# Row sums of 1024 columns: VectorE takes over the body, and the last row is divided differently

## The chip, the cores and the metric

The kernel runs on one core of a Trainium2 chip. The metric is the device time of one execution in microseconds (us). All times quoted are medians of fast runs; every run of this study was in the fast state, and the granted clock was 1.0 in all of them. One core does all the work, so there is no second core to compare with.

A profile shows one execution. Its span (162.4 us) is about 1.8 us shorter than the device time of the same execution. Below, DVE is VectorE, ACT is ScalarE, SP is SyncE, whose queue issues the loads and the store, and "landing" is the moment when the last of a load's 16 semaphore increments arrives (the core has 16 DMA engines, and the packet records show one increment behind each of 16 strings of packets). Where the text gives a landing that no copied line shows, it was read from the semaphore records of the trace.

## The reference

```python
x = np.random.randn(32, 512, 1024).astype(np.float32)     # 67.1 MB
out = np.sum(x, axis=-1)                                  # 32 x 512, 64 KB
```

There is one addition for each 4 bytes that are read. The 16384 rows are divided over 128 partitions, 128 rows on each.

## The kernel before

Eight tiles of 16 rows per partition (8.39 MB each) pass through a pool of three buffers. Each whole tile is divided equally: VectorE reduces rows 0 to 7 in one instruction, ScalarE sums rows 8 to 15 one by one, with a copy that also accumulates. The eighth tile is loaded in ever smaller pieces, so that little work is left when the last data land.

```python
xpool = ctx.enter_context(tc.tile_pool(name="x", bufs=3))
# ... cut: rows_dve = tensor_reduce over n rows; rows_act = one activation with accum_out per row
for t in range(T - 1):                       # seven whole tiles
    c0 = t * G
    xt = xpool.tile([P, G * D], F32, tag="xt", name="xt")
    load(xt, c0, 0, G * D)
    rows_dve(xt, c0, 0, G // 2)
    rows_act(xt, c0, G // 2, G // 2)
# ... cut: the last tile is loaded as 8, 4, 2 and 1 rows; then the last row as 512, 256 and 256 columns
for j, n in runs:
    if n > 1:
        rows_dve(xt, c0, j, n // 2)
        rows_act(xt, c0, j + n // 2, n // 2)
    else:
        rows_act(xt, c0, j, 1)
acc = [part[:, 0:1], part[:, 1:2], res[:, C - 1 : C]]
for i, (a, b) in enumerate(zip(cuts, cuts[1:])):     # three pieces of the last row, in a chain
    pairs_dve(xt, a, b, acc[i - 1] if i else 0.0, acc[i])
nc.sync.dma_start(out=out2d, in_=res)
```

`pairs_dve` is a `tensor_tensor_reduce`: it adds the two halves of a piece element by element and accumulates the sums. Each of the three calls starts from the result of the one before.

Of the kernel before, what the change touches and what calls it, by code (L numbers as in the profile page):

```python
# [1 line left out]

# [4 lines left out]

F32 = mybir.dt.float32
ADD = mybir.AluOpType.add


@with_exitstack
def kernel(
    ctx: ExitStack,
    tc: tile.TileContext,
    x: bass.AP,
    out: bass.AP,
):
    nc = tc.nc
    P = nc.NUM_PARTITIONS  # L20

    x_flat = x.flatten_outer_dims()
    R, D = x_flat.shape
    assert R % P == 0
    C = R // P

    x_p = x_flat.rearrange("(p c) d -> p (c d)", p=P)
    out2d = out.rearrange("a (b c) -> (a b) c", c=C)

    G = 16  # L30
    assert C % G == 0
    T = C // G

    xpool = ctx.enter_context(tc.tile_pool(name="x", bufs=3))
    rpool = ctx.enter_context(tc.tile_pool(name="res", bufs=1))
    res = rpool.tile([P, C], F32, name="res")
    part = rpool.tile([P, 4], F32, name="part")

    def load(xt, c0, a, b):
        nc.sync.dma_start(out=xt[:, a:b], in_=x_p[:, c0 * D + a : c0 * D + b])  # L40

    def rows_dve(xt, c0, j, n):
        nc.vector.tensor_reduce(  # L43
            out=res[:, c0 + j : c0 + j + n],
            in_=xt[:, j * D : (j + n) * D].rearrange("p (j d) -> p j d", d=D),
            axis=mybir.AxisListType.X,
            op=ADD,
        )

    def rows_act(xt, c0, j, n):  # L50
        for i in range(j, j + n):
            v = xt[:, i * D : (i + 1) * D]
            nc.scalar.activation(  # L53
                out=v,
                in_=v,
                func=mybir.ActivationFunctionType.Copy,
                accum_out=res[:, c0 + i : c0 + i + 1],
            )

    def pairs_dve(xt, a, b, first, acc):  # L60
        h = (b - a) // 2
        nc.vector.tensor_tensor_reduce(  # L62
            out=xt[:, a : a + h],
            in0=xt[:, a : a + h],
            in1=xt[:, a + h : b],
            scale=1.0,
            scalar=first,
            op0=ADD,
            op1=ADD,
            accum_out=acc,  # L70
        )

    for t in range(T - 1):
        c0 = t * G
        xt = xpool.tile([P, G * D], F32, tag="xt", name="xt")
        load(xt, c0, 0, G * D)
        rows_dve(xt, c0, 0, G // 2)
        rows_act(xt, c0, G // 2, G // 2)

    c0 = (T - 1) * G  # L80
    xt = xpool.tile([P, G * D], F32, tag="xt", name="xt")
    j = 0
    runs = []
    for n in (8, 4, 2, 1):
        load(xt, c0, j * D, (j + n) * D)
        runs.append((j, n))
        j += n
    cuts = [j * D + k for k in (0, D // 2, 3 * D // 4, D)]
    for a, b in zip(cuts, cuts[1:]):
        load(xt, c0, a, b)  # L90

    for j, n in runs:
        if n > 1:
            rows_dve(xt, c0, j, n // 2)
            rows_act(xt, c0, j + n // 2, n // 2)
        else:
            rows_act(xt, c0, j, 1)
    acc = [part[:, 0:1], part[:, 1:2], res[:, C - 1 : C]]
    for i, (a, b) in enumerate(zip(cuts, cuts[1:])):
        pairs_dve(xt, a, b, acc[i - 1] if i else 0.0, acc[i])  # L100

    nc.sync.dma_start(out=out2d, in_=res)


# [1 line left out]
_INS = ['x']  # L106
_OUTS = [((32, 512), 'float32')]


# [23 lines left out]
```

## Time and profile before

| kernel before | value | where it is read |
|---|---|---|
| time | 163.97 us (163.91 to 164.00, 4 runs) | runs |
| DMA in the chain that ended last | 85% | page |
| VectorE, ScalarE busy | 43%, 43% | page |
| time per whole tile in the stream | 19.4 us for 8.39 MB | windows |
| last data landed | 159.12 us | semaphore records |
| output store issued | 159.93 us | timeline |

These are two parts of the page, busy time by engine and the chain of work that ended last:

```profile
DVE 69.9 (43%) x16; ACT 69.0 (43%) x129; POOL 0.2 (0%) x4
...
DMA 85%; DVE 11%; SPq 1%; issue 1%; DVEq 0%
```

Both compute engines are idle for more than half of the time, and the chain is made of loads. The windows view over three whole tiles (columns: window and its length, busy time of each engine with its instructions, clock, DMA share, GB/s) tells the rate:

```profile
61.94:81.30 19.36, 8.69 (x1) 8.43 (x16) 0.00 (x0) 1.00 1.00 433
81.30:100.70 19.40, 8.69 (x1) 8.43 (x16) 0.00 (x0) 1.00 1.00 433
100.70:120.07 19.37, 8.69 (x1) 8.43 (x16) 0.00 (x0) 1.00 1.00 433
```

The 16 DMA engines are busy throughout (DMA share 1.00). In the packet records of this profile a 64 KB packet takes 2.42 us (median of 896; none took less than 2.415 us), and 16 x 64 KB in 2.42 us are 433 GB/s. So the body of the kernel waits for its loads, and these run without a gap. That they could not run faster is not shown by this.

What remains is the end. This is the timeline of the last 4 us, lines of ScalarE cut (columns: start, duration, engine, line, operation, operands; in brackets the idle time before it and what ended it):

```profile
156.55 1.22 DVE L43 TENSOR_REDUCE res<-xt 128x1 f32<-128x1024 f32 x1 [0.21 <-DMA xt<-in_x_dram]
...
158.64 0.42 DVE L62 CUSTOM_DVE_ANT_0 xt<-xt 128x256 f32<-128x256 f32 x1 [0.87 <-DMA xt<-in_x_dram]
...
159.11 0.35 DVE L62 CUSTOM_DVE_ANT_0 xt<-xt,part 128x128 f32<-128x128 f32 x1
159.38 0.08 DVE L62 DVE_READ_ACCUMULATOR2_ANT part<- 128x1 f32 x1
159.50 0.35 DVE L62 CUSTOM_DVE_ANT_0 xt<-xt,part 128x128 f32<-128x128 f32 x1
159.78 0.08 DVE L62 DVE_READ_ACCUMULATOR2_ANT res<- 128x1 f32 x1
159.93 0.35 SPq L102 DMA_DIRECT2D out_dram<-res  x1
```

The three chained operations on the last row start at 158.64, 159.11 and 159.50 us. The last data landed at 159.12, so the third operation started 0.38 us after its data were there, because it waited for the second.

### The profile page before, as it was taken

What the parts mean: (1) busy time and instruction counts of PE and PEld (TensorE: products, weight loads), DVE (VectorE), ACT (ScalarE), POOL (GpSimd) and SP (SyncE); (2) the same over time, 40 slices, a digit from 0 to 9 for tenths busy, and PEclk for the clock granted to TensorE, in tenths of its full rate; (3) what the DMA queues carried; (4) which work ended last, traced back from release to release, by engine and by line L of the source; (5) the groups of instructions that cost most, each with busy time, mean ns of one, the idle gap of its engine ahead of it and who ended that gap; (6) DMA issues with size and microseconds to landing.
All of it is one profiled execution on the core that took longest, in us unless ns stands there. A gap on an engine that the chain in (4) does not pass through costs nothing.

```text
span 162.4 us, 220 instructions
## 1 busy us (share of the span) xinstructions
DVE 69.9 (43%) x16; ACT 69.0 (43%) x129; POOL 0.2 (0%) x4
## 2 busy tenths in 40 slices
DVE  0000039700595007940099101990049700697882
ACT  3000039700594007930099101990039600696881
POOL 0000000000000000000000000000000000000000
DMA  7979989989989989989997997997997997999980
GB/s 258 517 323 452 517 355 420 517 371 404 501 355 436 517 371 404 517 371 404 517 452 325 517 468 307 517 468 323 501 484 323 484 484 307 452 420 408 418 350 20
DMA packets 2161, 67.18 MB, mean 414 GB/s; under 512 B 240, under 2 KB 624, under 8 KB 880
## 3 DMA queue, kind: packets, MB, share of 16 engines
q1 hardware_dynamic: 2160, 67.18, 96.3%
q14 instruction: 1, 0.01, 0.0%
HBM read 67.11 MB, written 0.07 MB: 414 GB/s over the span
## 4 chain that ended last, share of the span: by engine, by line
DMA 85%; DVE 11%; SPq 1%; issue 1%; DVEq 0%
DMA xt<-in_x_dram 85%; DVE res L43 11%; SPq L40 1%; DVE xt L62 0%; DVE part L62 0%; DVEq L62 0%; DVEq L128 0%
## 5 line engine op out<-in xcount | busy, mean ns | idle before, releaser
L43 DVE TENSOR_REDUCE res<-xt 128x8 f32<-128x8192 f32 (+3 forms) x10 | 68.7, 6873 | 89.0 <-DMA xt<-in_x_dram 89.0
L53 ACT ACTIVATE xt<-xt 128x1024 f32<-128x1024 f32 x64 | 66.7, 1043 | 89.3 <-DMA xt<-in_x_dram 89.1
L53 ACT ACTIVATION_READ_ACCUMULATOR xt<-xt 128x1 f32 x64 | 11.9, 187 | 0.0
L53 ACT ACT_TABLE_LOAD x1 | 1.3, 1283 | 0.7 <-PEq L117 0.7
L62 DVE CUSTOM_DVE_ANT_0 xt<-xt 128x256 f32<-128x256 f32 x1 | 0.4, 425 | 0.9 <-DMA xt<-in_x_dram 0.9
L62 DVE CUSTOM_DVE_ANT_0 xt<-xt,part 128x128 f32<-128x128 f32 x2 | 0.7, 352 | 0.1
L62 DVE DVE_READ_ACCUMULATOR2_ANT part<- 128x1 f32 x2 | 0.2, 82 | 0.0
L117 POOL MEMSET const-bfloat16-1.0<- 128x1 bf16 x1 | 0.1, 101 | 0.0
L117 POOL MEMSET const-uint8-127<- 128x1 uint8 x1 | 0.1, 101 | 0.0
L117 POOL MEMSET const-float32-0.0<- 128x1 f32 x1 | 0.1, 98 | 0.2 <-issue 0.2
L117 POOL MEMSET const-float32-1.0<- 128x1 f32 x1 | 0.1, 98 | 0.0
L62 DVE DVE_READ_ACCUMULATOR2_ANT res<- 128x1 f32 x1 | 0.1, 84 | 0.0
## 6 DMA issues: line engine op xcount, KB each, us to landing
xt<-in_x_dram SPq DMA_DIRECT2D x1, 4096.0 KB, 39.7
xt<-in_x_dram SPq DMA_DIRECT2D x1, 2048.0 KB, 44.2
xt<-in_x_dram SPq DMA_DIRECT2D x1, 1024.0 KB, 46.2
xt<-in_x_dram SPq DMA_DIRECT2D x1, 512.0 KB, 47.0
xt<-in_x_dram SPq DMA_DIRECT2D x1, 256.0 KB, 47.1
xt<-in_x_dram SPq DMA_DIRECT2D x2, 128.0 KB, 43.0
xt<-in_x_dram SPq DMA_DIRECT2D x7, 49.4
out_dram<-res SPq DMA_DIRECT2D x1, 64.0 KB, 1.5
```

The lines of the kernel that those rows point to most:

```text
L40: nc.sync.dma_start(out=xt[:, a:b], in_=x_p[:, c0 * D + a : c0 * D + b])
L43: nc.vector.tensor_reduce(out=res[:, c0 + j : c0 + j + n], in_=xt[:, j * D : (j + n) * D].rearrange("p (j d) -> p j d", d=D), axis=mybir.A ...
L53: nc.scalar.activation(out=v, in_=v, func=mybir.ActivationFunctionType.Copy, accum_out=res[:, c0 + i : c0 + i + 1],)
L62: nc.vector.tensor_tensor_reduce(out=xt[:, a : a + h], in0=xt[:, a : a + h], in1=xt[:, a + h : b], scale=1.0, scalar=first, op0=ADD, op1=A ...
L117: nc = _bacc.Bacc("TRN2", target_bir_lowering=False, num_devices=1)
```

## The change

VectorE sums whole tiles alone, with 16 rows in one instruction, and ScalarE joins only in the last whole tile (6 of 16 rows) and in the last tile. The last row is loaded in two pieces, 640 and 384 columns. VectorE and ScalarE each sum 320 columns of the first; their two partial sums are stored right behind the row's last column, so that one last VectorE reduction over 384 + 2 columns finishes the row. The intent: one chained operation fewer after the last landing.

```diff
-    for t in range(T - 1):
-        ...
-        rows_dve(xt, c0, 0, G // 2)
-        rows_act(xt, c0, G // 2, G // 2)
+        while c < whole:
+            ...
+            a = ACT_ROWS if final and c + m == whole else 0      # ACT_ROWS = 6
+            rows_dve(xt, res, 0, m - a, c)
+            rows_act(xt, res, m - a, a, c + m - a)
     # ... cut: the loads of 8, 4, 2 and 1 rows stay
-    cuts = [j * D + k for k in (0, D // 2, 3 * D // 4, D)]
-    for a, b in zip(cuts, cuts[1:]):
-        load(xt, c0, a, b)
+    nc.sync.dma_start(out=tail[:, 0:CUT], in_=x_b[:, last : last + CUT])      # CUT = 640
+    nc.sync.dma_start(out=tail[:, CUT:D], in_=x_b[:, last + CUT : last + D])
     # ... cut: rows of the last tile, divided as before; row 126 now goes to VectorE as 512 pairs
-    for i, (a, b) in enumerate(zip(cuts, cuts[1:])):
-        pairs_dve(xt, a, b, acc[i - 1] if i else 0.0, acc[i])
+    nc.vector.tensor_reduce(
+        out=tail[:, D : D + 1], in_=tail[:, 0 : CUT // 2], axis=X, op=ADD
+    )
+    sum_act(tail[:, CUT // 2 : CUT], tail[:, D + 1 : D + 2])
+    nc.vector.tensor_reduce(
+        out=res[:, n - 1 : n], in_=tail[:, CUT : D + 2], axis=X, op=ADD
+    )
```

More of the change, by code (lines that the diff above doesn't have):

```diff
@@ L9 @@
 ADD = mybir.AluOpType.add
+COPY = mybir.ActivationFunctionType.Copy
+X = mybir.AxisListType.X
+BLOCKS = (128,)
+G = 16
+ACT_ROWS = 6
+CUT = 640
 @with_exitstack
@@ L23 @@
     R, D = x_flat.shape
-    assert R % P == 0
     C = R // P
-    x_p = x_flat.rearrange("(p c) d -> p (c d)", p=P)
-    out2d = out.rearrange("a (b c) -> (a b) c", c=C)
-    G = 16
-    assert C % G == 0
-    T = C // G
+    assert R % P == 0 and sum(BLOCKS) == C
+    out_flat = out.rearrange("a (b c) -> (a b c)", c=1)
     xpool = ctx.enter_context(tc.tile_pool(name="x", bufs=3))
     rpool = ctx.enter_context(tc.tile_pool(name="res", bufs=1))
-    res = rpool.tile([P, C], F32, name="res")
@@ L37, with rows_dve @@
-    part = rpool.tile([P, 4], F32, name="part")
-    def load(xt, c0, a, b):
-        nc.sync.dma_start(out=xt[:, a:b], in_=x_p[:, c0 * D + a : c0 * D + b])
-    def rows_dve(xt, c0, j, n):
+    tail = rpool.tile([P, D + 2], F32, name="tail")
+    def rows_dve(xt, res, j, n, c):
         nc.vector.tensor_reduce(
-            out=res[:, c0 + j : c0 + j + n],
+            out=res[:, c : c + n],
             in_=xt[:, j * D : (j + n) * D].rearrange("p (j d) -> p j d", d=D),
-            axis=mybir.AxisListType.X,
+            axis=X,
@@ L47, in rows_dve @@
             op=ADD,
         )
-    def rows_act(xt, c0, j, n):
-        for i in range(j, j + n):
-            v = xt[:, i * D : (i + 1) * D]
-            nc.scalar.activation(
-                out=v,
-                in_=v,
-                func=mybir.ActivationFunctionType.Copy,
-                accum_out=res[:, c0 + i : c0 + i + 1],
-            )
-    def pairs_dve(xt, a, b, first, acc):
-        h = (b - a) // 2
-        nc.vector.tensor_tensor_reduce(
-            out=xt[:, a : a + h],
-            in0=xt[:, a : a + h],
-            in1=xt[:, a + h : b],
-            scale=1.0,
-            scalar=first,
-            op0=ADD,
-            op1=ADD,
-            accum_out=acc,
-        )
@@ L73 @@
-    for t in range(T - 1):
-        c0 = t * G
-        xt = xpool.tile([P, G * D], F32, tag="xt", name="xt")
-        load(xt, c0, 0, G * D)
-        rows_dve(xt, c0, 0, G // 2)
-        rows_act(xt, c0, G // 2, G // 2)
-    c0 = (T - 1) * G
-    xt = xpool.tile([P, G * D], F32, tag="xt", name="xt")
-    j = 0
-    runs = []
-    for n in (8, 4, 2, 1):
-        load(xt, c0, j * D, (j + n) * D)
-        runs.append((j, n))
-        j += n
-    cuts = [j * D + k for k in (0, D // 2, 3 * D // 4, D)]
@@ L89, with sum_act @@
-    for a, b in zip(cuts, cuts[1:]):
-        load(xt, c0, a, b)
-    for j, n in runs:
-        if n > 1:
-            rows_dve(xt, c0, j, n // 2)
-            rows_act(xt, c0, j + n // 2, n // 2)
-        else:
-            rows_act(xt, c0, j, 1)
-    acc = [part[:, 0:1], part[:, 1:2], res[:, C - 1 : C]]
-    for i, (a, b) in enumerate(zip(cuts, cuts[1:])):
-        pairs_dve(xt, a, b, acc[i - 1] if i else 0.0, acc[i])
-    nc.sync.dma_start(out=out2d, in_=res)
+    def sum_act(v, acc):
+        nc.scalar.activation(out=v, in_=v, func=COPY, accum_out=acc)
@@ new lines, in rows_act, with row_pairs_dve, block @@
+    def rows_act(xt, res, j, n, c):
+        for i in range(n):
+            sum_act(xt[:, (j + i) * D : (j + i + 1) * D], res[:, c + i : c + i + 1])
+    def row_pairs_dve(xt, res, j, c):
+        h = D // 2
+        a, b = xt[:, j * D : j * D + h], xt[:, j * D + h : (j + 1) * D]
+        nc.vector.tensor_tensor_reduce(
+            out=a, in0=a, in1=b, scale=1.0, scalar=0.0, op0=ADD, op1=ADD,
+            accum_out=res[:, c : c + 1],
+        )
+    def block(r0, n):
+        x_b = x_flat[r0 : r0 + P * n].rearrange("(p c) d -> p (c d)", p=P)
+        out_b = out_flat[r0 : r0 + P * n].rearrange("(p c) -> p c", p=P)
+        return x_b, out_b, rpool.tile([P, n], F32, name=f"res{r0}")
@@ new lines @@
+    r0 = 0
+    for b, n in enumerate(BLOCKS):
+        x_b, out_b, res = block(r0, n)
+        r0 += P * n
+        final = b == len(BLOCKS) - 1
+        whole = n - G - (n % G if final and n % G else 0) if final else n
+        c = 0
+        while c < whole:
+            m = min(G, whole - c)
+            xt = xpool.tile([P, G * D], F32, tag="xt", name="xt")
+            nc.sync.dma_start(out=xt[:, 0 : m * D], in_=x_b[:, c * D : (c + m) * D])
+            a = ACT_ROWS if final and c + m == whole else 0
+            rows_dve(xt, res, 0, m - a, c)
+            rows_act(xt, res, m - a, a, c + m - a)
+            c += m
+        if not final:
+            nc.scalar.dma_start(out=out_b, in_=res)
@@ new lines @@
+    xt = xpool.tile([P, G * D], F32, tag="xt", name="xt")
+    first = n - c - 8
+    cuts = [0, first, first + 4, first + 6, first + 7]
+    for i, k in zip(cuts, cuts[1:]):
+        nc.sync.dma_start(out=xt[:, i * D : k * D], in_=x_b[:, (c + i) * D : (c + k) * D])
+    last = (n - 1) * D
+    nc.sync.dma_start(out=tail[:, 0:CUT], in_=x_b[:, last : last + CUT])
+    nc.sync.dma_start(out=tail[:, CUT:D], in_=x_b[:, last + CUT : last + D])
+    for i, k in zip(cuts[:2], cuts[1:3]):
+        h = (k - i + 1) // 2
+        rows_dve(xt, res, i, h, c + i)
+        rows_act(xt, res, i + h, k - i - h, c + i + h)
@@ L106 @@
+    i = cuts[2]
+    rows_dve(xt, res, i, 1, c + i)
+    rows_act(xt, res, i + 1, 1, c + i + 1)
+    row_pairs_dve(xt, res, i + 2, c + i + 2)
+    nc.vector.tensor_reduce(
[5 more added lines that the diff above has]
+    )
+    nc.sync.dma_start(out=out_b, in_=res)
 _INS = ['x']
```

## The prediction

The sum along VectorE ends at 159.75 to 160.1 us against 159.85 before, so -0.10 to +0.25 us. Earlier landing would have taken up to 0.1 us off that; with this term the net was put at -0.3 to +0.3 us and the time at 163.85 us. The 267 ns in the pair operation are 256 columns at the fitted 1.067 us for 1024, an estimate.

> **What bounds the kernel now.** The DMA stream. The page's chain that ended last is 85% DMA, and DVE and ACT are each busy only 43%. In the timeline of VectorE the whole 16-row tiles start reducing at 42.27, 61.96, 81.33, 100.73, 120.09 and 139.44 us: (139.44 - 42.27)/5 = 19.43 us for 8.39 MB, so 432 GB/s. [...] Before each tile VectorE idles about 10.7 us, waiting for the load. Only what precedes the first load (about 2 us) and what follows the last landing can change.
>
> **Body.** VectorE's durations for 8, 4, 2 and 1 rows (8686, 4420, 2286, 1220 ns) fit 1.067 us a row plus 0.153 us. Sixteen rows are then an estimated 17.22 us, under the 19.43 us cadence. The 56 ScalarE rows of the seven body tiles become 6. The buffer is returned 17.2 us after a landing and not 8.7, but with three buffers there is still about 2 us of the next tile plus a whole tile (19.4 us) queued at that moment, so the stream should not starve. I expect issue-to-landing of a body load to fall from 49.4 to about 41 us and the cadence to stay at 19.4 us. [...]
>
> **Tail.** Now: the first piece of the last row releases VectorE at 158.47 us, its three chained pieces start at 158.64, 159.11 and 159.50 and end at 159.85, 1.4 us after that landing; the output is issued at 159.93 and the span ends at 162.4. After: VectorE is fully occupied from 139.44 on. Ten rows estimated 10.8 us (to 150.2), then 4 rows (to 154.6, landed at 154.05), 2 rows (to 156.8-157.0), 1 row (to 157.9-158.2), the pair op over 512 columns (425 ns for 256 plus 267, about 0.7 us and 0.1 for the accumulator, to 158.7-159.0), 320 columns (0.49 us, to 159.2-159.5), and the final 386 columns (0.56 us): end at 159.75 to 160.1. ScalarE's 320 columns [...] are done by about 159.2 and hide beside it. So the serial chain after the last data loses an op, but the 10-row share of VectorE leaves a small backlog that returns the gain. [...] Net: between -0.3 and +0.3 us, with the output store (about 2.5 us to the end) unchanged.
>
> **Prediction.** 163.85 us (before 163.96), 8 in 10 between 163.4 and 164.3. Chance of faster by over 2%: 0.01; within 2%: 0.98; slower by over 2%: 0.01.
>
> **What would show it.** VectorE busy near 134 us (about 82% of the span), ScalarE near 15 us; 16-row reduces of 17.2 us about 19.4 us apart, idle about 2.2 us between them, released by DMA; mean GB/s unchanged at about 414; in the last 20 us VectorE with almost no idle time from the 10-row op to the last, and the last VectorE op ending within 0.3 us of 159.85. If VectorE shows idle before the last op released by DMA or ScalarE, the backlog reading is wrong.
>
> **What would make it wrong.** The DMA queues running short because buffers come back 8.5 us later (cadence over 19.6 us, idle slices in the DMA row); sixteen-row reduces slower than fitted, over 19.4 us, which would make VectorE the bound; DMA speeding up without ScalarE's traffic; a backlog larger than reckoned, pushing the end over 160.2 us.

## The result

| | before | changed |
|---|---|---|
| time, us (runs) | 163.97 (163.91 to 164.00, 4) | 164.04 (163.91 to 164.13, 4) |
| ratio | | 1.0004, 95% interval 0.9987 to 1.0022 |
| last data landed, us | 159.12 | 159.14 |
| last VectorE operation on the row, start and duration, us | 159.50, 0.35 | 159.29, 0.55 |
| output store issued, us | 159.93 | 159.87 |

A ratio here is the mean time of one kernel's runs over that of the other's runs of the same rounds, so it is not quite the ratio of the medians. The result is 0.2 us from the predicted 163.85 us.

The same two parts of the page, for the changed kernel:

```profile
DVE 123.5 (76%) x14; ACT 15.8 (10%) x29; POOL 0.2 (0%) x4
...
DMA 75%; DVE 22%; SPq 1%; ACT 0%; issue 0%; ACTq 0%
```

VectorE does 1.8 times the work, ScalarE less than a quarter. VectorE's share of the chain rose from 11% to 22%, but this is not a new bound. The chain follows a load back to its issue, and the issue to the reduction that freed the buffer; that wait is in the chain although two other loads were queued meanwhile. The windows decide, over the same stretches:

```profile
61.94:81.30 19.36, 17.22 (x1) 0.00 (x0) 0.00 (x0) 1.00 1.01 433
81.30:100.70 19.40, 17.22 (x1) 0.00 (x0) 0.00 (x0) 1.00 1.00 432
100.70:120.07 19.37, 17.22 (x1) 0.00 (x0) 0.00 (x0) 1.00 1.00 433
```

The rate is the same with a 16-row reduction of 17.22 us beside it and no ScalarE work at all: 48 ScalarE instructions fewer in these three stretches changed it by nothing that can be read (432 to 433 GB/s against 433), and a 64 KB packet takes 2.42 us as before (median of 896).

The end of the changed kernel (in the first line four reductions, of 10, 4, 2 and 1 rows, are merged; lines of ScalarE before 158 us cut):

```profile
139.49 18.46 DVE L40 TENSOR_REDUCE res<-xt 128x10 f32<-128x10240 f32 x4 [2.12 <-DMA xt<-in_x_dram]
158.00 0.69 DVE L57 CUSTOM_DVE_ANT_0 xt<-xt 128x512 f32<-128x512 f32 x1
158.62 0.08 DVE L57 DVE_READ_ACCUMULATOR2_ANT res<- 128x1 f32 x1
158.69 0.47 ACT L48 ACTIVATE tail<-tail 128x320 f32<-128x320 f32 x1 [0.95 <-DMA tail<-in_x_dram]
158.69 0.49 DVE L102 TENSOR_REDUCE tail<-tail 128x1 f32<-128x320 f32 x1
159.07 0.19 ACT L48 ACTIVATION_READ_ACCUMULATOR tail<-tail 128x1 f32 x1
159.29 0.55 DVE L106 TENSOR_REDUCE res<-tail 128x1 f32<-128x386 f32 x1
159.87 0.35 SPq L109 DMA_DIRECT2D out_dram<-res  x1
```

The last operation starts 0.21 us earlier than its counterpart before (159.29 against 159.50), and it is 0.20 us longer (0.55 against 0.35). Its start has three conditions that fall close together: VectorE ends its 320 columns at 158.69 + 0.49 = 159.18, ScalarE's accumulator is read by 159.07 + 0.19 = 159.26, and the last load landed at 159.14. The chain view names ScalarE as the last of the three, and behind it the landing of the first piece at 158.67, for which ScalarE had been idle (a q behind an engine's name stands for its sequencer):

```profile
119.89 38.78 DMA tail<-in_x_dram
158.67 0.02 issue
158.69 0.47 ACT tail L48
159.16 0.10 ACTq L135
159.26 0.02 issue
159.29 0.55 DVE res L106
```

The prediction had said that a VectorE backlog would give the gain back, and that idle time before the last operation, ended by DMA or ScalarE, would contradict this. There is 0.11 us of it. So the time was right, and the reason for the tail was in doubt.

### The profile page after: what moved, and what is told of

It is laid out like the page before. It is cut to its first block, busy times and chain, and to the rows that moved or that the text cites. A ratio compares the mean times of both kernels' runs of the same rounds, so it can differ in the third digit from the quotient of the medians.

```text
span 162.4 us, 114 instructions
## 1 busy us (share of the span) xinstructions
DVE 123.5 (76%) x14; ACT 15.8 (10%) x29; POOL 0.2 (0%) x4
## 4 chain that ended last, share of the span: by engine, by line
DMA 75%; DVE 22%; SPq 1%; ACT 0%; issue 0%; ACTq 0%
DMA xt<-in_x_dram 51%; DMA tail<-in_x_dram 24%; DVE res L40 21%; SPq L89 1%; DVE res L106 0%; ACT tail L48 0%; SPq L77 0%; ACTq L135 0%
## 5 line engine op out<-in xcount | busy, mean ns | idle before, releaser
L40 DVE TENSOR_REDUCE res<-xt 128x16 f32<-128x16384 f32 (+4 forms) x10 | 121.8, 12204 | 36.2 <-DMA xt<-in_x_dram 36.2
L48 ACT ACTIVATE xt<-xt 128x1024 f32<-128x1024 f32 x13 | 13.6, 1045 | 2.9 <-DMA xt<-in_x_dram 2.9
L48 ACT ACTIVATION_READ_ACCUMULATOR xt<-xt 128x1 f32 x13 | 2.4, 187 | 0.0
L57 DVE CUSTOM_DVE_ANT_0 xt<-xt 128x512 f32<-128x512 f32 x1 | 0.7, 693 | 0.0
L106 DVE TENSOR_REDUCE res<-tail 128x1 f32<-128x386 f32 x1 | 0.6, 554 | 0.1
L48 ACT ACTIVATE tail<-tail 128x320 f32<-128x320 f32 x1 | 0.5, 469 | 1.0 <-DMA tail<-in_x_dram 1.0
L102 DVE TENSOR_REDUCE tail<-tail 128x1 f32<-128x320 f32 x1 | 0.5, 486 | 0.0
```

Source lines behind the costliest of these rows:

```text
L40: nc.vector.tensor_reduce(out=res[:, c : c + n], in_=xt[:, j * D : (j + n) * D].rearrange("p (j d) -> p j d", d=D), axis=X, op=ADD,)
L48: nc.scalar.activation(out=v, in_=v, func=COPY, accum_out=acc)
L57: nc.vector.tensor_tensor_reduce(out=a, in0=a, in1=b, scale=1.0, scalar=0.0, op0=ADD, op1=ADD, accum_out=res[:, c : c + 1],)
L102: nc.vector.tensor_reduce(out=tail[:, D : D + 1], in_=tail[:, 0 : CUT // 2], axis=X, op=ADD)
L106: nc.vector.tensor_reduce(out=res[:, n - 1 : n], in_=tail[:, CUT : D + 2], axis=X, op=ADD)
```

## The experiments

Theory 1 is that of the prediction: VectorE is late because of its ten rows of the last whole tile. Theory 2 comes from the two traces: there is no net backlog, the end is set by the last landing, and the change exchanges an earlier start of the last operation for a longer one.

A yardstick was needed first. Over all kernels whose body streams freely with three buffers, or with two in the kernel before, the last landing fell anywhere from 158.73 to 159.14 us. The changed kernel, profiled again, shows that this is not the edit:

> The changed kernel itself once more, as a scale for noise. The single profiles so far differ by up to 0.4 us in when the last data land (158.73 to 159.14 us) whatever the edit. If that is a property of the execution and not of the kernel, this profile will land its last data anywhere in about 158.7 to 159.2 us, and its last VectorE op will end 0.70 us after that, as in the first profile. If the changed kernel truly lands later than the others, it will be at about 159.1 us again and the time at about 164.05.

The repeated kernel landed its last data at 158.80 us and not 159.14, and issued the store at 159.55. Its time was 164.11 us against 164.13 us before (ratio 0.9995, interval 0.9982 to 1.0009, 6 runs). The landing therefore moves by 0.3 us without any edit, and a difference of that size between two single profiles proves nothing. (The sets of runs used different chips, so the chip may have a part in it; but the six runs of after2, all of one set, spread from 163.72 to 164.38 us.) The distance from last landing to store issue repeats within about 0.05 us and is used below.

| run | last landing, us | last operation: start, duration | store issued | landing to store, us | time, us | ratio to before (95%) |
|---|---|---|---|---|---|---|
| before | 159.12 | 159.50, 0.35 | 159.93 | 0.81 | 163.97 | 1 |
| bufs2_before | 158.73 | 159.11, 0.35 | 159.54 | 0.81 | 163.82 | 0.9991 (0.9971 to 1.0011) |
| body_only | 158.96 | 159.30, 0.35 | 159.73 | 0.77 | 163.75 | 0.9985 (0.9972 to 0.9999) |
| changed | 159.14 | 159.29, 0.55 | 159.87 | 0.73 | 164.04 | 1.0004 (0.9987 to 1.0022) |
| after2 | 158.80 | 158.97, 0.56 | 159.55 | 0.75 | 164.11 | 0.9995 (0.9982 to 1.0009) |
| tail_only | 158.94 | 159.08, 0.56 | 159.66 | 0.73 | 163.93 | 0.9992 (0.9979 to 1.0004) |
| act8 | 158.84 | 158.98, 0.56 | 159.57 | 0.73 | 163.84 | 0.9987 (0.9975 to 1.0000) |
| act4 | 158.75 | 160.80, 0.56 | 161.38 | 2.63 | 165.75 | 1.0104 (1.0090 to 1.0117) |
| cut768 | 158.87 | 159.24, 0.42 | 159.69 | 0.82 | 163.95 | 0.9989 (0.9975 to 1.0004) |
| final_short (wrong sums) | 158.86 | 159.01, 0.29 | 159.33 | 0.46 | 163.63 | 0.9973 (0.9959 to 0.9987) |
| final_pairs | 159.08 | 159.25, 0.36 | 159.65 | 0.57 | 163.89 | 0.9983 (0.9971 to 0.9995) |
| best | 158.81 | 158.97, 0.43 | 159.44 | 0.62 | 163.97 | 0.9988 (0.9973 to 1.0003) |

The kernel before had medians of 164.04, 164.01, 164.13 and 163.99 us in the four sets of runs; each ratio is to the runs of its own set. Distances are taken from the unrounded times.

One thing in the traces sharpens theory 2. With the changed tail the end hangs not on the last landing but on the one before it, that of the row's first piece (640 columns): it came at 158.67 us in the changed kernel, 158.35 in after2, 158.46 in tail_only and 158.36 in act8, and the store was issued 1.20 us later in each (1.198 to 1.202; the same in bufs2_after and start_split below). ScalarE sums its 320 columns from that landing on, the last operation waits for ScalarE, and by then the last piece has landed. From the last landing the same six profiles give 0.72 to 0.77 us. (With the tail before it is likewise the row's first piece, of 512 columns: the store follows it by 1.44 to 1.46 us in the three profiles.) Either way it is a landing and not a backlog that sets the end.

### Less work for VectorE: act8

```diff
-ACT_ROWS = 6
+ACT_ROWS = 8
```

> The changed kernel with ScalarE taking 8 and not 6 rows of the last whole tile, so that VectorE has two rows (2.13 us) less to do after 139.5 us. Theory 1 (on record in the prediction): the changed tail is shorter in itself, and a VectorE backlog returns the gain; then without the backlog the last VectorE op ends about 0.2 us before 159.84 us and the time falls by about 0.2 us. Theory 2 (from the two traces): there is no net backlog; the last data land at the same moment (159.12 us before, 159.14 us after), the last op starts 0.21 us earlier (159.29 against 159.50) but lasts 0.20 us longer (0.55 against 0.35); then the last op still cannot start before the landing at about 159.14, it starts at 159.2 to 159.3 and the time changes by less than 0.1 us. VectorE should now idle in the last 20 us, some 1.0 us before the 4-row reduce.

The timeline of VectorE now shows the gaps that the changed kernel lacks:

```profile
139.20 8.69 DVE L40 TENSOR_REDUCE res<-xt 128x8 f32<-128x8192 f32 x1 [2.13 <-DMA xt<-in_x_dram]
148.92 4.42 DVE L40 TENSOR_REDUCE res<-xt 128x4 f32<-128x4096 f32 x1 [1.03 <-DMA xt<-in_x_dram]
...
157.71 0.69 DVE L57 CUSTOM_DVE_ANT_0 xt<-xt 128x512 f32<-128x512 f32 x1 [0.19 <-DMA xt<-in_x_dram]
...
158.98 0.56 DVE L106 TENSOR_REDUCE res<-tail 128x1 f32<-128x386 f32 x1
```

VectorE idles 1.03 us before the 4-row reduction, so any backlog is gone. Still the last operation starts 0.14 us after the last landing (0.15 us in the changed kernel), and landing to store is 0.73 us, the same. The last operation did end 0.3 us earlier and the time was 0.2 us below before's, which is what theory 1 had named; but the landing in that profile is 0.30 us earlier too, and after2 shows that it moves so without any edit. The times alone can't tell (the interval of act8, 0.9975 to 1.0000, overlaps that of the changed kernel). Measured from the landing, taking the backlog away is worth nothing: theory 1 falls. The changed kernel had in fact caught up before its last operations: its pair operation on row 126 starts 0.14 us after that row landed at 157.86 us, as in act8 (0.14 us after 157.57).

### More work for VectorE: act4

```diff
-ACT_ROWS = 6
+ACT_ROWS = 4
```

> The changed kernel with ScalarE taking 4 and not 6 rows of the last whole tile: VectorE gets two more rows, 2 x 1.067 = 2.13 us. In the changed trace VectorE is done with its 320 columns at 159.18 us and waits 0.1 us for ScalarE's join. If VectorE is occupied without a gap from 139.5 us on, which both theories hold, the last op ends 2.0 to 2.1 us later, at about 161.9 us, and the time is about 166.1 us. If there were hidden slack in VectorE's run, the growth would be smaller by that slack.

VectorE and its last operation:

```profile
139.11 20.60 DVE L40 TENSOR_REDUCE res<-xt 128x12 f32<-128x12288 f32 x4 [2.17 <-DMA xt<-in_x_dram]
...
160.80 0.56 DVE L106 TENSOR_REDUCE res<-tail 128x1 f32<-128x386 f32 x1
```

Landing to store grew from 0.73 to 2.63 us, by 1.90 us for 2.13 us of added work, and the ratio is 1.0104. VectorE had about 0.23 us of slack from 139.5 us on (2.13 less 1.90). Six rows for ScalarE is thus close to the fewest that cost nothing: the next two rows on VectorE cost nearly their full length. This was expected to be 2.0 to 2.1 us; there was slightly more slack than that.

### Each half of the change alone: tail_only and body_only

```diff
 # tail_only: ScalarE takes 8 rows of every whole tile, tail as changed
-            a = ACT_ROWS if final and c + m == whole else 0
+            a = 8
 # body_only: on the kernel before; VectorE alone on tiles 0 to 5, tail as before
-        rows_dve(xt, c0, 0, G // 2)
-        rows_act(xt, c0, G // 2, G // 2)
+        n = G if t < T - 2 else G // 2
+        rows_dve(xt, c0, 0, n)
+        rows_act(xt, c0, n, G - n)
```

> The body of the kernel before (8 rows on each engine in all seven whole tiles) with the changed tail. Theory 1: last op about 0.2 us earlier than in the changed kernel, time about 163.8. Theory 2: last op starts at about 159.25 and ends at about 159.8, time within 0.1 us of both kernels. Neither expects the load cadence of 19.4 us to move. If ScalarE's 56 body rows slowed the loads, this kernel would be slower than the changed one by as much.

> VectorE alone on the first six whole tiles, the seventh split 8 and 8, then the tail of the kernel before. Both theories: the body change is worth nothing; cadence 19.4 us, last landing at about 159.1, the three chained ops of the last row end at about 159.85, time within 0.1 us of the kernel before. A theory that the body change had a gain of its own (fewer ScalarE writes) that the tail lost would have this kernel faster than before by 0.2 us or more.

The three profiles with the tail before have 0.81, 0.77 and 0.81 us from landing to store (mean 0.80), whichever body they have. The four with the changed tail and enough help from ScalarE have 0.73, 0.75, 0.73 and 0.73 (mean 0.73; bufs2_after and start_split below, which have the same tail, 0.72 and 0.77). So the body is worth nothing and the tail about 0.06 us, 0.04% of the time, with ranges that touch. The parts add up: measured from the last landing the last operation starts 0.22 us earlier on average and is 0.20 us longer, and the store follows its end by 0.03 us and not 0.07, where an accumulator had still to be read. body_only measured 0.15% below before, with an interval that ends at 0.9999. Its profile has its last landing between those of the other kernels and its landing to store at 0.77; nothing in it is faster than before except the landing, so no gain of the body is read from it.

### What the length of the last operation costs: final_short

This kernel gives a wrong result (the last row of each partition lacks 256 of its columns).

```diff
-        out=res[:, n - 1 : n], in_=tail[:, CUT : D + 2], axis=X, op=ADD
+        out=res[:, n - 1 : n], in_=tail[:, D - 128 : D + 2], axis=X, op=ADD
```

> Wrong on purpose: the last op of the changed kernel adds only the last 130 of its 386 columns, so the last row's sums are wrong; everything else stays. It measures what the length of that op costs. 256 columns fewer are 0.27 us on VectorE. Theory 2 (the gain went into the longer last op): the last op still starts at about 159.29 us, lasts about 0.29 us and not 0.55, and the time falls by about 0.27 us. If the end hung on anything else, the fall would be smaller.

```profile
159.01 0.29 DVE L106 TENSOR_REDUCE res<-tail 128x1 f32<-128x130 f32 x1
```

The operation fell from 0.554 to 0.289 us, by 0.265 us. Landing to store fell from 0.73 to 0.46 us, and the distance from the first piece's landing to the store from 1.198 to 0.933 us, by the same 0.265 us. The time fell too, 0.27% below before. The last operation's length lies fully on the critical path, so the 0.20 us by which the change lengthened it is where the 0.21 us of earlier start went. This is theory 2, with the first piece's landing in place of the last one.

### Moving the cut: cut768

```diff
-CUT = 640
+CUT = 768
```

> The changed kernel with the last row cut at 768 and not at 640 columns: the last op is down from 386 to 258 columns (0.42 us, 0.13 less), as much data in the last load as before, but the piece ahead of it is larger. Theory 2: the first piece lands about 0.15 us later (158.8), each engine then sums 384 columns (VectorE 0.55 us, ScalarE 0.52 us and 0.19 us), the last op starts at about 159.45 to 159.5 and ends at 159.85 to 159.9: what the last op gives, the join takes. Time within 0.1 us.

The last operation is 0.13 us shorter (0.42 us), and it starts 0.37 us after the landing and not 0.15, because each engine must first sum 384 columns (expected from VectorE's fit and, for ScalarE, from 0.469 us for 320 columns and 1.045 us for 1024 in the changed kernel's profile). Landing to store is 0.82 us, 0.09 longer. The cut trades one against the other, as expected; 640 is the better of the two.

### The margin of the loads: bufs2_after and bufs2_before

A buffer now comes back 17.2 us after its tile landed, and not 8.7. With three buffers that did no harm. With two it is a test of how early a load must be issued.

```diff
-    xpool = ctx.enter_context(tc.tile_pool(name="x", bufs=3))
+    xpool = ctx.enter_context(tc.tile_pool(name="x", bufs=2))
```

> The changed kernel with two and not three tile buffers. It tests the margin that the later return of a buffer uses up. A buffer returns 17.25 us after its tile landed, the next tile lands 19.4 us after that one, so about 2.1 us of loads are still queued when the next load is issued, and the first load of the kernel took 1.0 us from issue to its first packet and 2.2 us until the last of the 16 DMA engines had begun. Theory of the prediction (queue time left decides): just enough or slightly short, 164.0 to 165.5 us. Rival (a whole tile queued ahead is needed): over 2 us for each of five tiles, above 170 us.

> The kernel before with two tile buffers: the buffer returns 8.75 us after landing and leaves about 10.6 us of queued loads. Theory of the prediction: no change, 163.9 to 164.1 us. Rival (a whole tile queued ahead is needed): slower like the other two-buffer kernel.

The kernel before lost nothing (ratio 0.9991). The changed kernel took 170.23 us (169.66 to 171.42, ratio 1.0383, interval 1.0343 to 1.0423). Both named theories missed: it was not "just enough", and not every tile suffered. The timeline of VectorE with two buffers:

```profile
42.54 17.22 DVE L40 TENSOR_REDUCE res<-xt 128x16 f32<-128x16384 f32 x1 [2.35 <-DMA xt<-in_x_dram]
64.57 17.22 DVE L40 TENSOR_REDUCE res<-xt 128x16 f32<-128x16384 f32 x1 [4.81 <-DMA xt<-in_x_dram]
83.92 17.22 DVE L40 TENSOR_REDUCE res<-xt 128x16 f32<-128x16384 f32 x1 [2.13 <-DMA xt<-in_x_dram]
105.84 17.22 DVE L40 TENSOR_REDUCE res<-xt 128x16 f32<-128x16384 f32 x1 [4.70 <-DMA xt<-in_x_dram]
```

Every second tile comes about 22 us after the last and the others 19.35 us. The cause is in the lead of the issue. The load of the tile that landed at 64.55 us was issued at 40.22 us, 2.3 us before the previous landing at 42.52, and it took 24.3 us. The next was issued at 59.79 us, 4.8 us before the landing at 64.55, and then the stream had no gap. The packet records show the restart: packets of the late load begin between 41.4 and 43.5 us, and its first two rounds take mostly 2.7 to 3.7 us for 64 KB, where a packet in the stream takes 2.42 us. So the late load behaves like the very first load of the kernel, whose first packets took about 3.0 us (2.5 to 3.4 us in the kernel before). That the nearly empty queue is the reason for the long packets is argued and not shown: in start_split below a load that was issued about 40 us ahead also began with packets of 2.5 to 3.2 us. With three buffers the lead of a load is a whole tile more, 2.2 + 19.4 = 21.6 us.

### An attempt at the start: start_split

```diff
+            if c == 0:
+                h = P // 2
+                nc.sync.dma_start(out=xt[0:h, 0 : m * D], in_=x_b[0:h, c * D : (c + m) * D])
+                nc.scalar.dma_start(out=xt[h:P, 0 : m * D], in_=x_b[h:P, c * D : (c + m) * D])
```

> The changed kernel with its first load in two halves by partitions, issued at once from SyncE's and ScalarE's queues. In all profiles the 16 DMA engines begin their first packets one after the other, 1.7 to 2.9 us, and their last pieces land spread in the same way, 158.36 to 159.14 us. If the spread comes from one sequencer writing out the requests, two of them should halve it, the last landing comes 0.3 to 0.6 us earlier and the time falls as much. If it comes from elsewhere, the landing stays at 158.7 to 159.2 us and the time within 0.1 us.

(That one sequencer causes the spread is a supposition, put to the test here; no run shows it.) It failed: 183.88 us, ratio 1.1207. The engines' first packets still spread, from 2.05 to 3.50 us, and the first tile took nearly twice as long (landed at 43.29 us, against 23.15 in the changed kernel). Windows:

```profile
2.00:22.00 20.00, 0.00 (x0) 0.00 (x0) 0.00 (x0) 1.00 1.12 239
22.00:43.00 21.00, 0.00 (x0) 0.00 (x0) 0.00 (x0) 1.00 0.95 222
43.00:62.00 19.00, 17.22 (x1) 0.00 (x0) 0.00 (x0) 1.00 1.02 442
```

In the packet records all 16 engines take a packet of SyncE's queue together, then one of ScalarE's, in turn, and each 64 KB packet takes 4.93 us and not 2.42. So with two queues in turn, and each load covering 64 partitions and not 128, a packet of the same size took 4.93 / 2.42 = 2.04 times as long, and the rate fell to 222 to 239 GB/s; with the next loads, on one queue and over all 128 partitions, it was back at 442. Which of the two differences doubles the packet's time, and how, is not shown. Where the spread of the engines' starts comes from stays open.

### Pairs in the last operation: final_pairs and best

```diff
-    nc.vector.tensor_reduce(
-        out=res[:, n - 1 : n], in_=tail[:, CUT : D + 2], axis=X, op=ADD
-    )
+    h = (D + 2 - CUT) // 2
+    nc.vector.tensor_tensor_reduce(
+        out=tail[:, CUT : CUT + h], in0=tail[:, CUT : CUT + h], in1=tail[:, CUT + h : D + 2],
+        scale=1.0, scalar=0.0, op0=ADD, op1=ADD, accum_out=res[:, n - 1 : n],
+    )
```

> The changed kernel whose last op adds its 386 columns in pairs (193 against 193, as the kernel before adds pairs) instead of one after the other. The 256-pair op of the profile before took 0.425 us and the 128-pair op 0.352 us, plus 0.08 us for the accumulator read of which most overlaps; so an estimated 0.43 us from start to end of the read against 0.554. Theory 2: the end follows the last landing by about 0.58 us and not 0.70, time about 0.12 us less, which is near the noise of the times.

The last operation took 0.37 us to the end of its accumulator read (159.25 to 159.62) and not 0.55, and landing to store fell to 0.57 us, 0.16 us below the changed kernel:

```profile
159.25 0.36 DVE L107 CUSTOM_DVE_ANT_0 tail<-tail 128x193 f32<-128x193 f32 x1
159.54 0.08 DVE L107 DVE_READ_ACCUMULATOR2_ANT res<- 128x1 f32 x1
159.65 0.35 SPq L111 DMA_DIRECT2D out_dram<-res  x1
```

The time was 163.89 us, 0.9983 of before (0.9971 to 0.9995). It was combined with act8 and an earlier cut:

```diff
-ACT_ROWS = 6
-CUT = 640
+ACT_ROWS = 8
+CUT = 512
```

> The changed kernel with three edits: ScalarE takes 8 rows of the last whole tile, the last op adds in pairs, and the last row is cut at 512 and not 640 columns, so that the join of the first piece (measured ready 0.14 us after the last landing with 640) is ready with the landing. The last op then starts about 0.03 us after the last landing and takes about 0.43 us for 257 pairs: the end follows the landing by about 0.47 us, against 0.70 in the changed kernel, 0.73 in the one before and 0.54 with pairs alone. Theory 2 in full: nothing else can be had after the landing, so the time is about 0.25 us less than both, near 163.7, as far as the spread of landings (0.4 us) lets it be seen.

This missed: landing to store was 0.62 us, worse than pairs alone.

```profile
158.31 0.42 DVE L102 TENSOR_REDUCE tail<-tail 128x1 f32<-128x256 f32 x1
158.56 0.18 ACT L48 ACTIVATION_READ_ACCUMULATOR tail<-tail 128x1 f32 x1
158.97 0.43 DVE L107 CUSTOM_DVE_ANT_0 tail<-tail 128x257 f32<-128x257 f32 x1 [0.25 <-DMA tail<-in_x_dram]
```

Now both partial sums were ready (158.73 and 158.74), and the pair operation waited for the landing at 158.81 alone. It started 0.16 us after it, not the 0.03 us that was expected. In the chain of this run 0.05 us of that is VectorE's queue and 0.09 us issue. The kernel before shows the same: its first pair operation started at 158.64 us after a landing at 158.47, while a `tensor_reduce` starts 0.02 us after the landing that it waits for (139.49 after 139.47 in the changed kernel). With pairs alone the last operation also started 0.17 us after the last landing. So the cut at 512 bought no earlier start and cost 64 pairs. The time, 163.97 us (0.9988, 0.9973 to 1.0003), can't be told from before. The best version found is the changed kernel with pairs, by about 0.2%, at the edge of what the times can tell; the trace shows 0.16 us of it.

## Why the prediction was right, and where its reasons were not

- **Time.** Predicted 163.85 us (163.4 to 164.3); measured 164.04 us, ratio 1.0004.
- **Only what precedes the first load and what follows the last landing can change: right as far as the runs go.** What the runs show is that the rate stayed at 433 GB/s. The 16-row reduction took 17.22 us, exactly the estimate from 1.067 us a row plus 0.153 us. Issue to landing of a body load fell from 49.4 to 41.0 us (predicted about 41), VectorE's idle time before a tile to 2.1 to 2.3 us, and the mean stayed at 414 GB/s.
- **Three buffers suffice: right.** Two would not have: the expectation for that run (just enough or slightly short) was wrong, and it took 170.23 us.
- **VectorE busy near 134 us: wrong.** It was 123.5 us. The rows had been added up wrongly: VectorE has 6 x 16 + 10 + 4 + 2 + 1 = 113 whole rows, which make 113 x 1.067 + 10 x 0.153 = 122.1 us, plus the three operations on the two last rows. No conclusion rested on it.
- **End of the last operation between 159.75 and 160.1 us: right in the first profile**, at 159.84, but with luck: in after2, the same kernel, it ended at 159.52, because the data landed earlier. Luck also helped the sum along VectorE: its work without a gap ended at 159.18 us, and the path that really set the end, from the first piece's landing through ScalarE, released the last operation at 159.29.
- **"The 10-row share of VectorE leaves a small backlog that returns the gain": wrong.** This is the step that failed. With the backlog removed (act8) landing to store stayed at 0.73 us, and the store follows the first piece's landing by 1.20 us with and without it. What returned the gain is the length of the last operation, which stood in the prediction's sum (0.56 us) without being named as the cause: it starts 0.21 us earlier and is 0.20 us longer, and its length is on the critical path one for one (final_short: 0.265 us for 0.265 us). The net of the tail is about 0.06 us, far inside the spread of the last landing.
- **An earlier landing of the last data (a guess that no trace had shown): not seen.** 159.12 and 159.14 us in the first profiles, and landings from 158.73 to 159.14 over the kernels with either tail.

## What to carry to other kernels

Where the loads run without a gap from the first to the last, find the landing on which the end hangs, and measure only the distance from it to the final store: here it was the first of the row's two pieces, and the distance repeated within 0.01 us while the landing itself moved by 0.3. Work moved between engines that had idle time counted for nothing here (VectorE from 43% to 76% busy, ScalarE from 43% to 10%, the rate 433 GB/s in both). Taking an operation out of the final chain helps only if the one that remains is not made longer by the same amount (here 0.21 us earlier and 0.20 us longer). What runs after the last byte should have few elements: 256 columns fewer took 0.265 us off (final_short), and 193 pairs took 0.37 us where 386 columns took 0.55 (final_pairs). When an engine takes over work and returns a buffer later, compute how long before the previous landing the next load is then issued: here 2.3 us were too few and 4.7 us enough.

## What the traces measured beside the question

- How long ahead a load must be issued to keep the stream without a gap: for 8.39 MB loads (bufs2_after) an issue 2.0 to 2.3 us ahead of the previous landing lost 2.2 to 2.7 us, one 4.7 to 4.8 us ahead lost none. In the kernel before, the first packet of the first load began 1.0 us after the start of the issuing instruction (1.73 us after 0.73) and 0.63 us after its end at 1.11 us; the last engine's first packet began at 2.9 us, and first packets took about 3.0 us for 64 KB and not 2.42.
- The spread between the 16 DMA engines: the last load's increments arrived from 158.36 to 159.14 us in the changed kernel, so the slowest engine ended 0.8 us after the fastest.
- What VectorE took from a landing to the start of an operation: 0.02 us for `tensor_reduce`, 0.14 to 0.17 us for the pair operation (act8, body_only, best, before). Whether the operation or its number of waits is the cause was not tried.
- The change of the time of the last landing between executions of one kernel: 158.80 and 159.14 us for the same kernel, with the same granted clock. Whether both executions ran on one chip is not on record.
